# Identity products before waits that are foreseen, the page table at the fourth head, and an order written down, in a two-layer decoder step

## The chip, the cores and the metric

The kernel runs on one core of a Trainium2 chip. The metric is the device time of one launch in microseconds. A core has TensorE (matrix products into PSUM, an accumulator memory of eight banks), VectorE, ScalarE and GpSimd (elementwise work), SyncE (issues transfers), and DMA engines; each engine runs its own queue in order. ScalarE and GpSimd can issue transfers too.

## The reference

One inference step of two layers for a prompt of 512 tokens and eight samples of four tokens, width 1024, all in float32. Layer 0 mixes tokens with a gated linear recurrence (HGRN2, six heads of 128), layer 1 with sparse attention: an indexer scores all keys, the best 128 (prompt) or 256 (samples, over 1024 cached keys and the new ones) are chosen, and softmax attention runs over these. The samples' cached keys and values lie in pages that a page table names. Beside the mixer each layer has a cross-attention into 256 memory tokens, and behind it a gated MLP with a causal convolution of width 3.

```python
for layer in range(DEPTH):
    hp, hs = rms_norm(xp, norm_mix[layer]), rms_norm(xs, norm_mix[layer])
    if layer % N_MIXERS == 0:
        tp, sp = hgrn2_mixer(hp @ w_in_hgrn[j], s0, lower_bounds[j], hgrn_out_norm[j])   # and the samples
    else:
        ts = dsa_sample(qs, kn, vn, iqs, ikn, iws, cache_k[j], cache_v[j], cache_idx_k[j], page_table)
    xp = xp + jnp.concatenate([tp, cp], axis=-1) @ w_out[layer]
    fp, cvp = conv_ffn(rms_norm(xp, norm_ffn[layer]), ...)
    xp = xp + fp
```

## The kernel before

The stream is held feature-major, [128 features, 544 tokens] in eight tiles. A weight block of 128 x 1024 ("unit", 199 in all) is loaded by SyncE (in layer 1's mixer by GpSimd), cut by ScalarE into a rounded part `whi` and by VectorE or GpSimd into the rest `wlo`, and every product with the stream is three products of parts (`proj_fm`, lines 791 to 804): 48 products of 272 columns for one block of 128 features. Taking a unit into use cuts the unit two places later. An RMS norm is not applied before the product: `Norm._finish` (934 to 948) sums squares on TensorE, takes 1/sqrt by Newton steps on VectorE (`rsqrt`, 888), and turns the factor into rows by five transposes on TensorE (`rb`); the products are scaled as they leave PSUM (`scaled`, 950). In the MLP (`ffn`, 1180) the first gate and up blocks are computed before that factor is waited for.

The order of the instructions is made by the program. The main stream gives out the projections; beside it `Pump` (495) holds generators, each a chain of steps (a head's recurrence, a block of attention, a selection). Before each product of the main stream, `run` gives out all steps that `Model` (226), with a clock for each engine moved on by rough costs, holds ready; `finish`, `space` and `drain` do so until a generator ends or a tile is free. The same clocks choose the engine of some operations: VectorE or GpSimd for `wlo` (757), VectorE or ScalarE in `scale_rows` (861) and `scaled`. The program is made twice; the second time knows how often each tile is used.

Layer 0's mixer runs the parts of `MIX` (line 216): head 0, two blocks of values, the memory's keys and values, heads 1 to 4, another block of values, head 5, six gates. Then come the output projection (`out_proj`, 1172) and the MLP. Between the output projection and the MLP stand nine transfers of the page table, issued by ScalarE: 64 entries to all partitions (`ptb`, 1579) and, in eight pieces of 16 partitions, a strided copy (`ptv`, 1587), and on VectorE the six operations that make gather indices of them (`iidx`, `vidx`). The MLP of layer 0 gathers the index keys with `iidx`; layer 1 uses `vidx` and `ptb`.

Layer 1's mixer runs the parts of `ORDER` (line 217): index projections, memory loads, values, six queries, keys, then `attn` (adds the attention's generators), the memory's queries, and its keys and values. What is left of the attention is given out while the output projection waits for its inputs (`cat_ready`, 1168).

Of the kernel before, what the change touches and what calls it, by code (L numbers as in the profile page):

```python
# [33 lines left out]
# ---------------------------------------------------------------- host layout  # L34
# [43 lines left out]
def weight_units(i, order):  # L78
    """the weight blocks in the order in which the program asks for them"""
# [128 lines left out]
TURNS = 2          # selections at work at a time  # L208
# [10 lines left out]
ONACT = 4            # of a digit's seven thresholds, those that ScalarE counts  # L219
THRESHOLDS = 1, 2, 3, 4, 5, 6, 7  # L220

NUNITS = 199


class Model:
    """clocks of the engines (us), moved on by rough costs as instructions are given out, and the times from which
    tiles can be read: they decide which of the instructions at hand comes next"""
    LAT = dict(pe=0.2, act=0.14, dve=0.13, pool=0.1)     # from an instruction's end to a reader's start
    ROOM = dict(s=54, m=31, row=4, b=4)

    def __init__(self, plan=None):
        self.plan = plan                      # what an earlier pass wrote down; without it there is room for all
        self.uses, self.demand, self.pool, self.born, self.dies, self.held = {}, {}, {}, {}, {}, {}
        self.left, self.live = {}, dict.fromkeys(self.ROOM, 0)
        self.banks = [0.0] * self.ROOM["b"]   # times from which the free ones are free
        self.t = dict(pe=0.0, dve=0.0, act=0.0, pool=0.0, sp=0.0)
        self.dge, self.dma = [], []             # when the descriptor engine and the queues are busy
        self.ready, self.read, self.floor, self.rings = {}, {}, {}, {}
        self.whole = []
        self.lanes = [0.0] * 8, [0.0] * 8  # L240
        self.gen = None
        self.table, self.psum, self.mine, self.touch = 0, set(), {}, {}
        self.strict, self.keep, self.main = 2, 0, MAIN0
# [31 lines left out]
    def holds(self):  # L275
        """for each generator and step: the slots that it still takes at the most, and those that it gives back
        until its end"""
# [37 lines left out]
    def room(self, g, gens):  # L315
        """from when a generator's next step finds the tiles that it takes"""
# [12 lines left out]
    def ring(self, tag, n, name):  # L329
        """a tile takes the place of the one n allocations before it"""  # L330
# [11 lines left out]
    def held_up(self, n, eng):  # L342
        """until when other engines are at work on the part of a tile that is to be written"""
# [14 lines left out]
    def go(self, eng, cost, ins, outs):  # L358
# [3 lines left out]
        for n in outs:  # L362
            s = max(s, self.floor.get(n, 0.0))
            s = max(s, self.held_up(n, eng))
            if eng == "dve":
                s = max(s, self.mine.get(n, 0.0))
        e = self.t[eng] = s + cost
# [12 lines left out]
class Engine:  # L380
# [3 lines left out]
    def __getattr__(self, name):  # L384
        f = getattr(self._e, name)

        def call(*args, **kw):
# [9 lines left out]
            self._m.use(ins + outs)  # L397
            return f(*args, **kw)  # L398
# [3 lines left out]
def place(busy, t, took):  # L402
    """the first time from t on when something is free for so long"""
# [11 lines left out]
def extent(ap):  # L415
    """first and last column and partition of an operand in its tile"""
# [14 lines left out]
def cost(eng, model, name, args, kw, ins, outs):  # L431
    out = args[0] if args else kw["out"]
    n = size(out)
    if name in ("dma_start", "indirect_dma_start"):
        m = model
        at = m.t["pe"] if eng != "sp" or outs[0] not in m.floor else 0.0
        lanes = m.lanes[eng == "pool"]        # their completions are told apart by eight semaphores in turn
# [17 lines left out]
    if eng == "pe":  # L455
        l = args[1]
        load = size(l) * 0.107 / 128          # of the stationary operand, beside the product before
# [37 lines left out]
class Pump:  # L495
    """Generators of instructions beside the main stream. A generator yields, before each step, the tiles that
    the step reads (None: all that it has given out so far); a step is given out once they are ready."""
    def __init__(self, model):
        self.turn = 0
        self.m, self.gens, self.dv, self.names, self.urgent = model, [], [], {}, []  # L500

    def make(self, it, after=None, pri=0, margin=0):
        name = (self.m.gen.key + "_" if self.m.gen else "") + it.__name__
        self.names[name] = n = self.names.get(name, 0) + 1
        return Gen(it, after, f"{name}{n}", pri, margin)
# [12 lines left out]
    def ready(self, g):  # L518
# [5 lines left out]
        else:  # L524
            for n in g.need:
                if callable(n):                       # a condition, or a time
# [18 lines left out]
    def step_dve(self):  # L545
        """the streams take turns, so that one's instruction does not wait for its own one before"""
# [3 lines left out]
    def ahead(self):  # L550
        """steps of the DVE's own streams while it would otherwise wait"""
# [17 lines left out]
    def run(self, *need):  # L569
        """all steps that are ready; then, until the main stream's needs are ready, those that become so"""  # L570
# [13 lines left out]
    def idle(self):  # L584
        """nothing is ready: wait for what comes first; False if nothing can"""
# [14 lines left out]
    def finish(self, g):  # L600
        while not g.done:
# [8 lines left out]
    def space(self, tag):  # L610
        """the main stream's own tiles: it leaves some for the generators as long as they get on"""
# [8 lines left out]
    def drain(self):  # L620
        while self.gens:
# [3 lines left out]
def program(ctx, tc, a, pat, cat_, order, plan):  # L625
# [34 lines left out]
    def v3(ap, *dims):  # L660
        """[P, prod(dims)] -> [P, *dims]"""
# [53 lines left out]
    # ---- weights: loaded ahead in the order of their use, cut into two float32r parts  # L715
    class Weights:
        def __init__(self):
# [3 lines left out]
            self.whole = list(plan.whole) if plan else []       # units that are also used as they are  # L721
# [18 lines left out]
        def _cut(self):  # L740
# [12 lines left out]
            def part(c, n):  # L753
                S.activation(hi[:, c:c + n], raw[:, c:c + n], AF.Copy)
                late = max(model.t["pe"], model.t["pool"]) + self.lead
                (V if model.t["dve"] <= late else G).tensor_sub(lo[:, c:c + n], raw[:, c:c + n], hi[:, c:c + n].bitcast(F32))
# [3 lines left out]
            else:  # L760
                self.part = part              # the first unit is cut block by block
# [24 lines left out]
    def mm3(out, wh, wl, xh, xl, first, last):  # L786
        """out += x^T w, weights moving, both operands in two parts; three of the four products carry float32"""
# [3 lines left out]
    def proj_fm(blocks, xs, ks=None):  # L791
        """feature-major product: blocks() gives the next [128,128] weight parts, xs is a list of (hi, lo)"""
# [18 lines left out]
    def fm2(*name, xs, before=None, ks=range(8)):  # L811
        """two feature-major products, block by block"""
# [22 lines left out]
    def proj_tm(*name, xs):  # L835
        """token-major product with 256 columns, the results of the four prompt tiles and, for the samples, of
        the four blocks of a unit on 32 rows each"""
# [23 lines left out]
    def scale_rows(p, r):  # L861
        if model.t["act"] < model.t["dve"]:
# [10 lines left out]
    def split_in(src):  # L873
        """the two parts of a slot's contents as a generator"""
# [6 lines left out]
    def split2(src, parts, sl):  # L881
        """the same as a generator"""
# [5 lines left out]
    def rsqrt(v, out=None, p=128):  # L888
        """1/sqrt(v) by Newton steps on an integer first guess; v is overwritten"""
# [17 lines left out]
    # ---- residual stream, feature-major [d, token], and its norms: h holds x * gain in two parts,  # L907
    #      the factor 1/rms of a token is applied to the products
# [1304 lines left out]
```

## Time and profile before

| what | us |
|---|---|
| median of three runs (lowest, highest) | 1495.1 (1492.55, 1497.12) |
| span of the profiled execution | 1500.7 |
| TensorE busy in it | 1434.9 (96%) |
| VectorE, ScalarE, GpSimd busy | 803.2, 587.5, 567.3 |
| mean granted clock of TensorE, share of full | 0.978 |

The profiled execution is another one than the three timed ones; of its own time only the span from the first to the last instruction is given. Busy times overlap, since the engines run side by side. Layer 0's mixer takes about the first 287 us with its memory attention, its MLP begins at about 340 us; layer 1's mixer lies between about 747 and 1050 us, and its MLP follows from about 1102. The clock of TensorE is shown as a share of its full speed. All operations are recorded at one helper line (L398), so rows are told apart by their tiles: `a` is a projection's accumulator, `rb` and `rs` belong to a norm, `wlo` and `whi` to the weights.

### The profile page before, as it was taken

To read this page: it belongs to the slowest core of one execution; us is meant where nothing else is said; L and a number is where in the kernel's file an instruction comes from. 1 tells how busy PE (TensorE), PEld (TensorE's weight loads), DVE (VectorE), ACT (ScalarE), POOL (GpSimd) and SP (SyncE) were. 2 spreads that over 40 slices of the span, in tenths; PEclk is the share of its full clock that TensorE was granted. 3 is DMA by queue.
4 is the path that set the end of the run, shared out by engine and by line. 5 is a ranking of instruction groups with operands and counts; after the bars stand their busy time and mean duration, and the time that the engine had idled before them with its cause. 6 is when DMAs were issued, how large, how long until landed. Compare 5 with 4: busy or idle time off the path is not lost.

```text
span 1500.7 us, 28191 instructions
## 1 busy us (share of the span) xinstructions
PE 1434.9 (96%) x11314; PEld 1345.6 (90%) x11314; DVE 803.2 (54%) x1762; ACT 587.5 (39%) x1064; POOL 567.3 (38%) x600
## 2 busy tenths in 40 slices
PE   8989999998999999999999797689999999999998
PEld 7978889998999999999987775456999999999998
DVE  7466886653444234444469988867444442244431
ACT  5447466332333123333335443466333331133320
POOL 4422444323444124446753444341134440144410
PEclk9999999999999999999999997989999999999999
DMA  5542132321333223224414236631222323232241
GB/s 186 177 156 64 59 117 86 101 85 62 88 95 93 92 73 94 90 85 126 135 54 131 83 115 202 199 127 57 71 76 89 96 85 99 73 95 87 85 121 57
DMA packets 60145, 152.52 MB, mean 102 GB/s; under 512 B 9040, under 2 KB 22960, under 8 KB 60016
## 3 DMA queue, kind: packets, MB, share of 16 engines
q1 hardware_dynamic: 39456, 110.11, 23.9%
q0 software_dynamic: 8208, 26.50, 5.4%
q10 hardware_dynamic: 12352, 14.13, 2.9%
q8 instruction: 89, 1.46, 0.4%
q14 instruction: 40, 0.33, 0.1%
HBM read 142.23 MB, written 8.47 MB: 100 GB/s over the span
## 4 chain that ended last, share of the span: by engine, by line
PE 84%; DVE 11%; issue 2%; ACT 1%; DMA 1%; another core or an unknown queue 0%; ACTq 0%; POOL 0%; SPq 0%; DVEq 0%; POOLq 0%
PE a L398 71%; DVE ple_choose_sample L398 2%; PE u_hgrn_head L398 1%; DVE isc_index_prompt L398 1%; PE id_index_prompt L398 1%; PE mkv L398 1%; PE ao_prompt_attn L398 1%; PE ho_hgrn_head L398 1%; PE ms_prompt L398 1%; PE hgrn_head_samples L398 1%; PE as_prompt_attn L398 1%; DVE t L398 1%; DMA ptv<-pt 1%; DVE lo L398 1%; PE mo_prompt L398 1%
## 5 line engine op out<-in xcount | busy, mean ns | idle before, releaser
L398 PE MATMUL a<-hi,whi 128*128 128x272 f32 x2640 | 556.4, 292 | 1.4 <-DVE t L398 1.0
L398 PE MATMUL a<-lo,whi 128*128 128x272 f32 x2640 | 551.0, 290 | 4.9 <-DVE lo L398 4.6
L398 POOL TENSOR_TENSOR wlo<-raw,whi 128x1024 fp32r<-128x1024 f32 x143 | 342.7, 2397 | 557.3 <-ACT whi L398 551.1
L398 PE MATMUL a<-hi,wlo 128*128 128x272 f32 x2640 | 549.1, 289 | 0.0
L398 PEld LDWEIGHTS a<-hi,whi 128*128 128x128 f32 x2640 | 417.7, 190 | 9.2 <-issue 5.4
L398 PEld LDWEIGHTS a<-lo,whi 128*128 128x128 f32 x2640 | 418.1, 190 | 6.2 <-DVE lo L398 5.6
L398 PEld LDWEIGHTS a<-hi,wlo 128*128 128x128 f32 x2640 | 418.1, 190 | 0.0
L398 ACT ACTIVATE whi<-raw 128x1024 fp32r<-128x1024 f32 (+1 forms) x202 | 209.5, 1038 | 230.9 <-PE a L398 151.3
L398 DVE TENSOR_TENSOR wlo<-raw,whi 128x1024 fp32r<-128x1024 f32 (+1 forms) x59 | 79.7, 1351 | 160.6 <-ACT whi L398 157.7
L398 DVE TENSOR_TENSOR sc<-a,rb 128x544 f32<-128x544 f32 x53 | 38.4, 724 | 116.1 <-PE a L398 114.5
L398 DVE SCALAR_TENSOR_TENSOR conv<-ext,params,conv 128x560 f32<-128x560 f32 x88 | 70.6, 802 | 45.1 <-ACT conv L398 43.6
L398 DVE TENSOR_TENSOR ext<-a,rb 128x240 f32<-128x240 f32 x132 | 37.5, 339 | 105.9 <-PE a L398 102.2
L398 ACT ACTIVATE conv<-ext,params 128x560 f32<-128x560 f32 x44 | 37.6, 855 | 136.2 <-DVE ext L398 132.6
L398 ACT ACTIVATE hi<-sc 128x544 fp32r<-128x544 f32 x44 | 29.0, 658 | 137.3 <-DVE sc L398 137.3
L398 DVE TENSOR_TENSOR x<-a,x 128x544 f32<-128x544 f32 x48 | 34.7, 723 | 80.1 <-PE a L398 72.5
L398 POOL TENSOR_TENSOR sqa<-sqa,sq 128x544 f32<-128x544 f32 x24 | 34.8, 1448 | 110.0 <-ACT sq L398 108.3
L398 DVE TENSOR_TENSOR sc<-sc,conv 128x512 f32<-128x512 f32 x88 | 62.5, 748 | 4.9 <-DVE sc L398 0.5
L398 ACT ACTIVATE conv<-conv 128x560 f32<-128x560 f32 x44 | 29.6, 672 | 73.8 <-DVE conv L398 73.8
L398 ACT ACTIVATE hi<-x,params 128x544 fp32r<-128x544 f32 x32 | 23.9, 745 | 70.4 <-DVE x L398 68.5
L398 DVE TENSOR_TENSOR lo<-sc,hi 128x544 fp32r<-128x544 f32 x44 | 31.9, 725 | 31.9 <-ACT hi L398 31.9
L398 PE MATMUL a<-whi,hi 128*128 128x256 f32 x160 | 46.8, 293 | 0.0
L398 PE MATMUL a<-whi,lo 128*128 128x256 f32 x160 | 45.1, 282 | 0.0
(406 smaller groups left out, 1931.9 us busy)
## 6 DMA issues: line engine op xcount, KB each, us to landing
raw<-w SPq DMA_DIRECT2D x177, 512.0 KB, 3.6
raw<-w POOLq DMA_DIRECT2D x21, 512.0 KB
k_sample_scores<-ckT SPq DMA_DIRECT2D x46, 128.0 KB, 3.5
ck_mem_samples<-cmkT ACTq DMA_DIRECT2D x16, 256.0 KB, 6.2
cv_mem_samples<-cmv ACTq DMA_DIRECT2D x16, 256.0 KB, 4.7
st_s<-hgrn_head_samples POOLq DMA_DIRECT2D x12, 256.0 KB
hgrn_head_samples<-hst SPq DMA_DIRECT2D x10, 256.0 KB, 3.5
ck_sample_scores<-ckT SPq DMA_DIRECT2D x18, 128.0 KB, 2.1
```

The costliest lines, as they stand in the source:

```text
L398: return f(*args, **kw)
```

## The change

Three parts. First, the page table's nine transfers become a function that is called where head 3 of layer 0 begins, and the six index operations move ahead of the output projection. Second, the order of layer 1 is read from a string: letters name generators in the order in which they are made, a point ends the turn of `run`, `finish`, `space` or `drain`, and `+` or `-` answers a choice of engine (`pick`). Third, in layer 1's mixer up to the output projection, before the first product into a PSUM tile of 128 partitions (or a transpose) for which `Model` computes a wait of over 0.8 us, products of the identity with itself are given out that write the same tile.

```diff
+SCRIPT = (
+    "5.-A6.A2.-2.A8.-5.-2B2.B5.B3.-.B9.-4.B.B9.-CD6.3C.16C2E12CE2CE4CF4CE8CD2C4DFEF2D.-EFEDFH.HEF.E.FE.F.EF.EF.EF6.-I"
...
+    "-8.+8.+8.+8.-8.+24."
+)
 class Model:
+        if eng == "pe":
+            self.wait, self.last = s - self.last, s + cost
 class Engine:
             self._m.use(ins + outs)
+            out = args[0] if args else kw["out"]
+            if self._n == "pe" and self._m.fill and self._m.wait > 0.8 and out.shape[0] == 128 and (
+                    name == "transpose" or kw["start"]):
+                self._m.fill(out, self._m.wait)
             return f(*args, **kw)
 class Pump:
+    def begin(self, script):
+        self.made = [*self.gens, *self.dv]
+        self.script = iter([c for n, c in re.findall(r"(\d*)(\D)", script) for _ in range(int(n or 1))])
+    def play(self):
+        for c in self.script:
+            if c == ".":
+                return
+            g = self.made[LETTERS.index(c)]
+            self.step(g, self.gens if g in self.gens else self.dv)
+    def pick(self, c):
+        return c if self.script is None else next(self.script) == "+"
     def run(self, *need):
+        if self.script is not None:
+            return self.play()
...
-                (V if model.t["dve"] <= late else G).tensor_sub(lo[:, c:c + n], raw[:, c:c + n], hi[:, c:c + n].bitcast(F32))
+                (V if pump.pick(model.t["dve"] <= late) else G).tensor_sub(lo[:, c:c + n], raw[:, c:c + n], hi[:, c:c + n].bitcast(F32))
...
+    def page_table():
+        pt_ap = a["pt"]
+        S.dma_start(ptb, bass.AP(tensor=pt_ap.tensor, offset=pt_ap.offset, ap=[[0, 128], [1, 64]]))
+        for s in range(8):
+            S.dma_start(ptv[16 * s:16 * s + 16, :], bass.AP(tensor=pt_ap.tensor, offset=pt_ap.offset + s, ap=[[0, 16], [8, 8]]))
...
         hd = int(part)
+        if hd == 3:
+            page_table()
         f = fm("hfm", TOK + 128 * hd, xs=h)
...
+    if plan is not None:
+        pump.begin(SCRIPT)
     h = norm.h
...
+    def fill(out, us):
+        out = out[:, 0:min(size(out), 128)]
+        for _ in range(int((us - 0.4) / 0.224)):
+            nc.tensor.matmul(out, ident, ident[:, 0:size(out)], start=True, stop=True, skip_group_check=True)
+    model.fill = fill
     model.keep, model.main = KEEP, MAIN1
     for part in ORDER:
...
     W.queue, W.lead = Q, LEAD0
+    model.fill = None
```

## Rows read from the trace of the kernel before

**Rows 1.** The page: its span, and each engine's busy time.

```profile
span 1500.7 us, 28191 instructions
...
PE 1434.9 (96%) x11314; PEld 1345.6 (90%) x11314; DVE 803.2 (54%) x1762; ACT 587.5 (39%) x1064; POOL 567.3 (38%) x600
```

**Rows 2.** Windows: stretch, length, busy PE, PEld, DVE, ACT, POOL; clock, DMA, GB/s.

```profile
350.00:400.00 50.00, 47.43 (x359) 46.98 (x360) 23.93 (x55) 16.42 (x22) 19.19 (x26) 0.93 0.24 77
150.00:200.00 50.00, 47.85 (x446) 43.03 (x445) 42.38 (x113) 28.47 (x62) 22.27 (x26) 1.00 0.23 80
```

**Rows 3.** Windows of layer 1's mixer, with the same columns.

```profile
889.50:893.00 3.50, 3.50 (x26) 1.98 (x25) 3.03 (x16) 2.75 (x10) 0.00 (x0) 0.54 0.98 381
910.00:920.00 10.00, 5.42 (x18) 4.06 (x15) 9.75 (x35) 1.01 (x2) 4.28 (x6) 0.51 0.53 171
927.00:934.00 7.00, 5.85 (x20) 3.87 (x24) 4.44 (x18) 1.69 (x2) 1.68 (x4) 0.53 0.89 285
```

**Rows 4.** Waits, 340 to 400 us: total, times, longest, in us.

```profile
DVE vidx L398 <- DMA ptv<-pt: 10.0, 1, 10.0
...
PE rb__finish L398 <- DVE rs L398: 5.1, 1, 5.1
```

**Rows 5.** Timeline of TensorE, 346 to 358 us: start, length; idle time before in brackets.

```profile
352.57 1.36 PE L398 MATMUL rb__finish<-consts,rs 128*128 128x128 f32 x5 [5.05 <-DVE rs L398]
353.86 0.82 PE L398 MATMUL a<-hi,whi 128*128 128x272 f32 x2
...
357.83 0.41 PE L398 MATMUL a<-hi,whi 128*128 128x272 f32 x2
```

**Rows 6.** Windows of TensorE's work on `a` alone, from the norm's sums on, both MLPs.

```profile
339.76:379.76 40.00, 32.96 (x247) 0.91 0.22 71
...
1101.96:1141.96 40.00, 38.58 (x305) 1.00 0.27 80
```

**Rows 7.** Timeline of TensorE, layer 1's MLP: the factor's transposes.

```profile
1105.96 0.77 PE L398 MATMUL rb__finish<-consts,rs 128*128 128x128 f32 x5
```

**Rows 8.** The page table's tiles: count, shortest/median/longest in ns, first and last start.

```profile
L398 ACTq DMA_DIRECT2D ptv<-pt x8: 441/452/516, 336.2 to 339.7; - x8
...
L398 DVE TENSOR_SCALAR iidx<-ptb,consts x2: 233/238/242, 339.2 to 339.4; 64x32 int32<-64x32 int32 x2
```

**Rows 9.** Timeline of ScalarE, 138 to 215 us.

```profile
140.67 1.05 ACT L398 ACTIVATE whi<-raw 128x1024 fp32r<-128x1024 f32 x1
...
174.40 0.45 ACT L398 ACTIVATE oss_hgrn_head<-hgrn_head_samples 128x128 f32<-128x128 f32 x2 [6.52 <-PE hgrn_head_samples L398]
...
181.75 1.05 ACT L398 ACTIVATE whi<-raw 128x1024 fp32r<-128x1024 f32 x1
```

**Rows 10.** Waits of TensorE, 138 to 300 us: the only one.

```profile
PE u_hgrn_head L398 <- DVE km_hgrn_head L398: 2.2, 1, 2.2
```

**Rows 11.** SyncE: its wait in 336 to 345 us, and its timeline in 142 to 148.

```profile
SPq L398 <- DMA ptv<-pt: 7.5, 1, 7.5
...
144.27 0.33 SPq L398 DMA_DIRECT2D raw<-w  x1
```

**Rows 12.** Timeline of GpSimd at the end: a weight's second part.

```profile
1449.61 2.40 POOL L398 TENSOR_TENSOR wlo<-raw,whi 128x1024 fp32r<-128x1024 f32 x1 [12.53 <-ACT whi L398]
```

**Rows 13.** Waits of TensorE, 747 to 940 us.

```profile
PE qrb_query_scale L398 <- DVE rq L398: 3.3, 1, 3.3
PE mb_mem_samples L398 <- POOL rqx_mem_samples L398: 2.0, 1, 2.0
...
PE a L398 <- DVE t L398: 1.0, 1, 1.0
```

**Rows 14.** Float32 products, two records each: chain row at full clock, timeline row at half.

```profile
204.47 0.89 PE u_hgrn_head L398 x8
...
911.45 1.01 PE L398 MATMUL e_choose_sample<-ple_choose_sample,consts 128*128 128x2 f32 x4 [1.37 <-DVE ple_choose_sample L398]
```

**Rows 15.** Waits of VectorE, 885 to 951 us.

```profile
DVE p_prompt_attn L398 <- PE as_prompt_attn L398: 3.5, 1, 3.5
```

More of the change, by code (lines that the diff above doesn't have):

```diff
@@ L1 @@
+import re
 import numpy as np
@@ L222 @@
 NUNITS = 199
+LETTERS = "ABCDEFGHIJKLMNOPQRSTUVWXYZabcdefghijklmnopqrstuvwxyz!#$%&()*,/:;<=>?@[]^_{|}~"
+SCRIPT = (
+    "5.-A6.A2.-2.A8.-5.-2B2.B5.B3.-.B9.-4.B.B9.-CD6.3C.16C2E12CE2CE4CF4CE8CD2C4DFEF2D.-EFEDFH.HEF.E.FE.F.EF.EF.EF6.-I"
+    "2JHEHIJ.HF.E.FE.FE.FE.F.EF4.-2.J2H2.J3.J4.-2.J2H2.J3.J5.-2HK.K5.HEFH.K4.-2.2H10.-.2H15.-M2HL.L7.-HEFEHLM4.F.EFM"
+    "10.NMNJ2H.-VX2OZabcdePQRSTUW.J.OJ2.JHEFH2.J.2O.-2H.3J.J4.J6.2fOJ3.-f3JHJHJO.f.J6.-4J3OJEJFf3P3Q3R2S2T2U.2J6.-JPQ"
+    "STRU.S.EFJTU.EF.EP-3.-Q-JR+PS-T-U+fJ.QRPF2J.EfJFEfFQREJS.FE2f2PJ2Q2RP3SQT5.GRUglSFGFGJFP-Q-TGP2Tg3Jf.-JPQR+S-T3U"
+    "QfJF2GJfGPQT+U2WPVfPQP+RSU-VTgGQ2h2i2j2kP2G2RV-RSGSQ+VG2VGVPGRWQSTGR+2TXSQTRS+UWXR2GX+ST-3U4WTGUXGXG2XSGU+TGhiUh"
+    "jUGWi2Wh+-jki+-2h2WiGhj2-kW3Yih2-jijhk-+i2-jh3Gi3Yhi3G3Yij+-2kjGkGjG2P2Q2RP2SP+Q2TR2US2YPQ-TU3YQR-S-jk2-lYPZT-RU"
+    "-QZaSRZabTSabcUTbcdkUc.delkdel.k3.e3l9.+19.+11.+11.+11.+11.+11.+14.-m6.m2.-2.m10.-2.-10.-9.-2.-10.-9.-2.-10.-9.-"
+    "2.-10.-9.-2.-10.-9.-2.-10.-9.-2.-10.-9.-2.-10.-9.-2.-10.-9.-2.-10.-9.-2.-8.+8.+8.-8.+8.+8.+8.-8.+8.+8.+8.-10.-9."
+    "-2.-10.-9.-2.-10.-9.-2.-10.-9.-2.-10.-9.-2.-10.-9.-2.-10.-9.-2.-10.-9.-2.-10.-9.-2.-10.-9.-2.-10.-9.-2.-8.+8.+8."
+    "-8.+8.+8.+8.-8.+24."
+)
 class Model:
@@ L241, in __init__ @@
         self.gen = None
+        self.fill, self.wait, self.last = None, 0.0, 0.0
         self.table, self.psum, self.mine, self.touch = 0, set(), {}, {}
@@ L499, in __init__ @@
         self.turn = 0
+        self.script, self.made = None, []
         self.m, self.gens, self.dv, self.names, self.urgent = model, [], [], {}, []
@@ L504, in make @@
         self.names[name] = n = self.names.get(name, 0) + 1
-        return Gen(it, after, f"{name}{n}", pri, margin)
+        g = Gen(it, after, f"{name}{n}", pri, margin)
+        self.made.append(g)
+        return g
+    def begin(self, script):
[9 more added lines that the diff above has]
+        return c if self.script is None else next(self.script) == "+"
     def add(self, it, after=None, pri=5, margin=0):
@@ L600, in finish @@
     def finish(self, g):
+        if self.script is not None:
+            return self.play()
         while not g.done:
@@ L610, in space @@
     def space(self, tag):
+        if self.script is not None:
+            return self.play()
         m = self.m
@@ L620, in drain @@
     def drain(self):
+        if self.script is not None:
+            return self.play()
         while self.gens:
@@ L861, in scale_rows @@
     def scale_rows(p, r):
-        if model.t["act"] < model.t["dve"]:
+        if pump.pick(model.t["act"] < model.t["dve"]):
             S.activation(p, p, AF.Copy, scale=r)
@@ L951, in scaled @@
         t = slot(name="sc")
-        if model.t["dve"] > max(model.t["pe"], model.t["act"]) + BUSY:
+        if pump.pick(model.t["dve"] > max(model.t["pe"], model.t["act"]) + BUSY):
             S.activation(halves(t), ac, AF.Copy)
@@ L1542, in gate @@
         cat[hd] = yield from split_in(sg)
+    ptb = cp.tile([128, 64], I32, name="ptb")
+    ptv = cp.tile([128, 8], I32, name="ptv")
+    def page_table():
[3 more added lines that the diff above has]
+            S.dma_start(ptv[16 * s:16 * s + 16, :], bass.AP(tensor=pt_ap.tensor, offset=pt_ap.offset + s, ap=[[0, 16], [8, 8]]))
     memraw = []
@@ L1573, in program @@
         gens.append(pump.add(hgrn_head(hd, q, f, lb, m, lambda n: vts[n], ons), after=gens[hd - FLIGHT] if hd >= FLIGHT else None, pri=PRI["hg"], margin=MARGIN))
-    norm = Norm(gffn[:, 0, :])
-    out_proj(0, cat, [*([g] for g in gates), [mg[0], mg[1], mg[4]], mg[2:5]], norm)
-    n1 = Norm(gmix[:, 1, :])
-    ptb = cp.tile([128, 64], I32, name="ptb")
-    pt_ap = a["pt"]
-    S.dma_start(ptb, bass.AP(tensor=pt_ap.tensor, offset=pt_ap.offset, ap=[[0, 128], [1, 64]]))
     iidx = cp.tile([128, 32], I32, name="iidx")
@@ L1585, in program @@
         V.tensor_scalar(iidx[pr], p4[pr, :, e], 64.0, cc("iota64")[pr], op0=ALU.mult, op1=ALU.add)
-    ptv = cp.tile([128, 8], I32, name="ptv")
-    for s in range(8):
-        S.dma_start(ptv[16 * s:16 * s + 16, :], bass.AP(tensor=pt_ap.tensor, offset=pt_ap.offset + s, ap=[[0, 16], [8, 8]]))
     vidx = cp.tile([128, 4, 8], I32, name="vidx")
@@ L1592, in program @@
         V.tensor_scalar(vidx[:, i, :], vidx[:, 0, :], float(i), None, op0=ALU.add)
+    norm = Norm(gffn[:, 0, :])
+    out_proj(0, cat, [*([g] for g in gates), [mg[0], mg[1], mg[4]], mg[2:5]], norm)
+    n1 = Norm(gmix[:, 1, :])
     def gather(out, src, idx):
```

## The prediction

> **What bounds the kernel now.** I read the page first: it puts TensorE's busy share of the 1500.7 us at 96% [rows 1], so time goes where TensorE stands still or runs at its lower clock. The windows come next. Three places concern this change: the start of layer 0's MLP (350 to 400 us: TensorE 47.43 of 50 busy, mean granted clock 0.93) and the stretch where head 3 begins (150 to 200: 47.85 busy, VectorE 42.38) [rows 2], and layer 1's mixer, where the clock is low again and again while VectorE is full (9.75 of 10 us in 910 to 920) [rows 3]. The waits of 340 to 400 us name the cause in the first: VectorE stands 10.0 us for the last page-table transfer, and TensorE 5.1 us for the norm factor that is queued behind this on VectorE [rows 4]. The chain of waits runs through the same transfer.
>
> **The page table moves.** *Removed, in layer 0's MLP.* The index operations sit on VectorE ahead of the norm's Newton steps; without them these follow the sums at once. The timeline of TensorE shows what the delay costs: 5.05 us idle before the five transposes of the factor, these 1.36 us long, and then products at two thirds to half speed (a pair takes 0.82, 0.41 once the clock is back) until 357.8 us [rows 5]. The clock was at 2.4 GHz, fell to 1.2 GHz after the idle time, and rose again. The price of the whole is read from the same step in layer 1, where nothing stands before the norm: in the 40 us from the sums on, TensorE does 305 products there and 247 here, 38.58 us for 305, that is 0.126 each [rows 6]. 58 products x 0.126 = 7.3 us. It agrees with the pieces: 5.05 idle, 0.6 on the transposes (1.36 against 0.77 [rows 7]), 1.6 on some 16 products at half speed. What is late next is known from layer 1 too: the transposes follow the products without idle time, so nothing takes the stall's place. Lower bound of the gain: 5.05, if another low clock comes; upper: 7.3. I take 7.3.
>
> *Added, at head 3 in layer 0.* Nine transfers are issued by ScalarE just before head 3's first product: some 9 x 0.45 = 4.1 us with what lies between them [rows 8]. Each unit of weights that is taken into use has the cut of the one two places later ahead of it; counted back from the third block of values, head 3's first is taken with the cut at 140.67 us [rows 9], and the nine come just before, ahead of this cut, the copies out of the memory attention and head 2's activations. ScalarE next stands idle for long before 174.4 us (6.52 us [rows 9]), so up to there what it feeds may be late. The cut is for a block that comes into use two units later and has time; the copies release PSUM and feed VectorE, which is almost full there. The trace holds no such hold-up in the mixer, so bounds: nothing, if TensorE has products of heads 2 and 3 to do meanwhile (the planner of layer 0 is still at work and counts ScalarE late by about as much, so it gives those out first); 4.1 idle and 2.2 for the lower clock as after the idle time at 350 us (0.6 + 1.6 above), 6.3, if all of it reaches TensorE; below nothing, -2.2, if the new order avoids the one wait of 2.2 us that TensorE has there [rows 10]. I take +1.5: nearer the busy TensorE row than the full hold-up. The transfers' own way: SyncE stood 7.5 us behind them in the stretch from 336 us. At 144.27 SyncE issues a weight load [rows 11]; the same wait would put it to about 152, for a block that ScalarE cuts some 30 us later, at 181.75 [rows 9]: nothing.
>
> The Trainium skill ("DMA: Bandwidth & Descriptors", "Issuing engines are not separate DMA queues") says that transfers of ScalarE and SyncE end up on the same engines and interleave, which speaks against putting these beside head 3's weight and state loads. The 7.5 us of SyncE agree that one issuer's small transfers hold up another's. By the rule a load is late; by the slack of 30 us it costs nothing.
>
> *The index operations.* Six, the longest of 0.24 us [rows 8], at most 1.4 us, go ahead of the output projection, whose VectorE work waits for TensorE; their data has landed long before. 0, at most 1.4.
>
> **The order written down.** Read mark by mark, the string gives out layer 1 exactly as the planner of before does: the same 975 turns of the main stream, the same generator steps between, the same 36 and 122 choices of engine. The trace shows this where a choice has its own row: the string's last marks are + + - + + + - +, and the last eight weight parts of the trace are cut on VectorE twice, on GpSimd (1449.61), then three on VectorE, one on GpSimd, one on VectorE [rows 12]. 0, with no bound on either side but the fills.
>
> **The fills.** They are 128 x 128 products of float32 identities, before the first product into a PSUM tile of 128 partitions (or a transpose) where the program's own clocks see a wait over 0.8 us, (wait - 0.4)/0.224 each. They act only until the output projection begins, at about 951 us here; the waits of the attention after that get none. In the trace the longest waits that qualify are 3.3 us (query scale) and 2.0 (memory queries), and there is one of 1.0 for an accumulator [rows 13]: 12 + 7 + 2 = 21 products if the clocks saw them as the chip has them; with the shorter ones and waits that the chip doesn't have I allow 20 to 40. One costs 0.22 us (four in 0.89), 0.45 at the lower clock (two of the same kind 1.01) [rows 14]. Cover: the waits themselves. Not covered: the accumulator's, because a fill writes the very bank whose release is awaited and so starts after the wait (2 x 0.22 = 0.45); and any that the clocks foresee where the chip has no wait, such as the turn of the keys.
>
> What they give back: the low stretches within their reach are 889.5 to 893 (clock 0.54), 910 to 920 (0.51) and 927 to 934 (0.53) [rows 3]. (1 - clock) x length is 1.6, 4.9 and 3.3. The second is free: VectorE is busy 9.75 of 10 and TensorE 5.42, so VectorE sets the pace. The others, 4.9 together, are on the path: VectorE stands 3.5 us for the score products that come at the end of the last stretch [rows 15]. Bounds: -4.9; and +8.8 for 40 uncovered products at 0.22, +18 at 0.45. I take -1.0: a fifth of the gain kept after 0.5 of uncovered fills and half a microsecond where fills outlast the 2.0 us wait. The Trainium skill ("TensorE: Matmul & The Clock Gate", "HAM oscillation — how this bites in real kernels") counts half of all throttled time as lost. By it these stretches would give back half of 20.5 us, 10; the row that shows VectorE full takes the middle one out of that.
>
> **Sum.** -7.3 + 1.5 + 0 + 0 - 1.0 = -6.8 us. Of the profiled execution only the span is given, 1500.7, 3.6 above the slowest of the three timed runs (1492.55 to 1497.12); so the difference is carried to the median: 1495.1 - 6.8 = **1488.3**.
>
> **Rivals.**
> 1. *ScalarE's hold-up at head 3 reaches TensorE.* For: VectorE is nearly full and takes its input from ScalarE there. Against: TensorE waits but once between 138 and 300 us. -7.3 + 6.3 - 1.0: 1493.1.
> 2. *The fills hold the clock up.* For: the low stretch of 927 to 934 follows the wait of 2.0 us that is filled. Against: fills take a third of the 3.3 us wait if foreseen short. -7.3 + 1.5 - 4.9: 1484.4.
> 3. *The stall's place is taken.* The MLP's weight parts or accumulators are late instead, half of 7.3 goes. For: the idle row there names only what came last, and a second lateness can lie behind it. Against: layer 1's rows. -3.7 + 1.5 - 1.0: 1491.9.
> 4. *The fills lie on the path: slower.* They wait for the bank, run at the lower clock, and the queue is in order, so scores, memory keys and VectorE behind them are late. 40 x 0.45 = 18, less the 5.8 of the table: 1507. It decides from 13 uncovered fills at the lower clock or 26 at the upper. For: the clock is low in 17 of the 24 us from 910 to 934. Against: most are put where TensorE has an idle row.
>
> **How the numbers follow.** Forecast 0.50, rival 1 0.18, rival 2 0.14, rival 3 0.10, rival 4 0.08. The forecast's own range is 1485 to 1491.5. The range for 8 in 10 leaves out rival 4 and the edges of 2 and 1: 1481.5 to 1495.0. 0.3% of 1495.1, 4.5 us, is what a measurement here can tell from no change: faster is below 1490.6. Faster: nearly all of rival 2 and 0.46 of the forecast with little of rival 3, 0.63; same: rivals 1 and 3 and the forecast's rest, 0.28; slower 0.09.
>
> **What would show it.** The wait of VectorE for the page table is gone and the transposes of layer 0's MLP factor follow about 4 us after the sums without idle time; the windows behind stay at clock 1.00. ScalarE shows nine issues near 141 us and TensorE's idle time in 138 to 175 stays below 4 us. Between 820 and 951 us there are 20 to 40 identity products; the clock of 927 to 934 tells rival 2 from the forecast. From 1050 us on the kernel takes as long as before. The forecast fails if layer 0 ends over 4 us later than before, or if TensorE's fills stand where it had no idle time.

## The result, and the profile after: slower by half a per cent

The changed kernel takes **1502.2 us** (median of 12 runs, 1499.65 to 1504.9), the kernel before 1494.2 on the same chip (12 runs, 1488.2 to 1497.12): a ratio of **1.0056, 95% interval 1.0043 to 1.0068**. It is slower by 8 us where 6.8 us less was forecast.

The page of the changed kernel: its span and each engine's busy time, against [rows 1].

```profile
span 1501.1 us, 28288 instructions
...
PE 1446.2 (96%) x11370; PEld 1358.1 (90%) x11370; DVE 816.5 (54%) x1763; ACT 586.1 (39%) x1063; POOL 566.1 (38%) x599
```

The spans of the two profiled executions hardly differ, since before's is 6.5 us above its median and the changed kernel's 1.1 below. So the stages are compared, each from the sums of one norm (the first `st__finish` product) to the next:

| stage, us | before | after | difference |
|---|---|---|---|
| up to layer 0's first norm | 26.0 | 26.7 | +0.7 |
| layer 0's mixer and output projection | 313.4 | 328.6 | **+15.2** |
| layer 0's MLP | 407.6 | 399.7 | **-7.9** |
| layer 1's mixer and output projection | 354.8 | 346.2 | -8.6 |
| layer 1's MLP | 398.9 | 400.0 | +1.1 |

All but layer 1's mixer add up to +9.1, about what the medians show. Layer 1's mixer varies most between profiles of one kernel (the changed kernel has 346.2 here and 360.4 on another chip, e5 below); it is left to the experiments.

**The MLP of layer 0 did what was foreseen.** Windows of the changed kernel with the columns of [rows 2]: from 350 us on TensorE is busy all the time at full clock, where before had 47.43 and 0.93. The second row is `a` alone from the sums on: 306 products in 40 us, against 247 [rows 6].

```profile
350.00:400.00 50.00, 50.00 (x407) 49.76 (x405) 22.09 (x48) 17.60 (x23) 18.94 (x23) 1.00 0.28 89
```

```profile
355.25:395.25 40.00, 38.58 (x306) 1.00 0.25 80
```

The timeline of TensorE there: the factor's transposes come 4.15 us after the sums, without idle time, and take 0.77 us instead of 1.36 [rows 5].

```profile
355.24 1.12 PE L419 MATMUL st__finish<-consts,sqa 128*128 128x1 f32 x16
...
359.14 0.41 PE L419 MATMUL a<-hi,wlo 128*128 128x272 f32 x2
359.39 0.77 PE L419 MATMUL rb__finish<-consts,rs 128*128 128x128 f32 x5
```

**The mixer of layer 0 lost twice that.** Windows of the whole stage, up to 138 us (just before head 3) and from there on; first the kernel before:

```profile
25.99:138.00 112.01, 107.86 (x849) 94.11 (x849) 65.59 (x171) 57.07 (x118) 36.87 (x40) 0.98 0.42 135
138.00:339.39 201.39, 199.24 (x1742) 185.33 (x1737) 140.68 (x337) 107.12 (x215) 77.25 (x69) 1.00 0.27 86
```

and the changed kernel, with the 50 us in which head 3 begins [rows 2]:

```profile
26.65:138.00 111.35, 107.32 (x825) 93.27 (x824) 62.65 (x166) 54.11 (x112) 36.86 (x40) 0.95 0.40 131
138.00:355.25 217.25, 208.47 (x1765) 191.65 (x1764) 156.55 (x348) 109.55 (x221) 75.64 (x69) 0.98 0.26 83
```

```profile
150.00:200.00 50.00, 46.20 (x392) 40.63 (x392) 41.96 (x97) 26.27 (x58) 18.86 (x18) 0.93 0.18 60
```

Two numbers of such a row say what it loses: length less busy TensorE is idle time, and (1 - clock) x length what the lower clock costs. The clock is shown to 0.01, so the second number is good to about 1 us in such a stretch. From 138 us on, before has 2.1 + 0.0, the changed kernel 8.8 + 4.3. What is left of the stage once both losses are taken off in both parts is 304.9 before and 305.9 after: the same work. So some 11.0 of the 15.2 us are new waits of TensorE, and the low clock behind them, from head 3 on. Another 3.3 are low clock ahead of 138 us (5.6 against 2.2), where both kernels give out the same instructions; the runs below show anything from 2.2 to 6.7 there, whatever their order, so it is put down to chance.

The waits of TensorE from 138 to 305 us (total, times, longest). Before has one, of 2.2 [rows 10]:

```profile
PE ot_hgrn_head L419 <- DVE o_hgrn_head L419: 2.0, 1, 2.0
PE hgrn_head_samples L419 <- DVE km_hgrn_head L419: 1.9, 1, 1.9
PE ho_hgrn_head L419 <- DVE hgrn_head_samples L419: 1.5, 1, 1.5
PE sc_hgrn_head L419 <- DVE k_hgrn_head L419: 1.2, 1, 1.2
PE u_hgrn_head L419 <- ACT on_hgrn_head L419: 0.9, 2, 0.7
```

Only the fourth stands near ScalarE's nine issues, and e2 below has it without them. The issues are there, at 142 us; the timeline of ScalarE:

```profile
142.09 0.33 ACTq L419 DMA_DIRECT2D ptb<-pt  x1
142.46 0.45 ACTq L419 DMA_DIRECT2D ptv<-pt  x1
...
144.38 2.86 ACTq L419 DMA_DIRECT2D ptv<-pt  x6
147.29 1.06 ACT L419 ACTIVATE whi<-raw 128x1024 fp32r<-128x1024 f32 x1 [3.53 <-PE mpt_prompt L419]
```

Right behind them the order on TensorE is another. Before (timeline of TensorE), three rows of head 3's f projection, six products, stand between the memory attention's transposes and its last products:

```profile
143.10 0.50 PE L398 MATMUL a<-hi,whi 128*128 128x272 f32 x2
...
143.69 0.41 PE L398 MATMUL a<-hi,wlo 128*128 128x272 f32 x2
144.04 2.00 PE L398 MATMUL mo_prompt<-mpt_prompt,mv 128*64 128x256 f32 x16
```

In the changed kernel it is 18 rows, 36 products, from 146.10 on: five blocks more, since three rows are a block of the product. The attention's last products and head 2's recurrence (`sc_hgrn_head`) come behind them, and then TensorE has to wait:

```profile
146.10 0.50 PE L419 MATMUL a<-hi,whi 128*128 128x272 f32 x2
...
150.45 0.41 PE L419 MATMUL a<-hi,wlo 128*128 128x272 f32 x2
150.79 2.00 PE L419 MATMUL mo_prompt<-mpt_prompt,mv 128*64 128x256 f32 x16
152.72 0.65 PE L419 MATMUL mot_join<-consts,mo_mem_samples 128*128 128x128 f32 x4
153.22 0.39 PE L419 MATMUL sc_hgrn_head<-sc,kd_hgrn_head 128*128 128x128 f32 x2
154.83 0.33 PE L419 MATMUL sc_hgrn_head<-consts,k_hgrn_head 128*128 128x128 f32 x1 [1.23 <-DVE k_hgrn_head L419]
```

The planner has been told of nine issues on ScalarE, some 4.3 us by its own costs, holds the generators' steps behind ScalarE for not ready, and gives out these five blocks ahead of them. From there on the order of layer 0 is new: of the 1554 turns, steps and choices of engine that the planner makes for it, the first 333 are as before.

Three of the four longest waits stand right behind VectorE operations that took several times their usual length beside operations of GpSimd; the rows are in the last section. The fourth, the 1.5 us at 223 us, has GpSimd idle.

### The profile page after: what moved, and what is told of

It reads as the page before. It is cut to its first block, busy times and chain, and to the rows that moved or that the text cites. A ratio compares the mean times of both kernels' runs of the same rounds, so it can differ in the third digit from the quotient of the medians.

```text
span 1501.1 us, 28288 instructions
## 1 busy us (share of the span) xinstructions
PE 1446.2 (96%) x11370; PEld 1358.1 (90%) x11370; DVE 816.5 (54%) x1763; ACT 586.1 (39%) x1063; POOL 566.1 (38%) x599
## 4 chain that ended last, share of the span: by engine, by line
PE 81%; DVE 13%; ACT 3%; issue 2%; DMA 1%; POOL 0%; SPq 0%; DVEq 0%; ACTq 0%; POOLq 0%
PE a L419 70%; DVE ple_choose_sample L419 2%; PE mkv L419 1%; DVE isc_index_prompt L419 1%; DVE m_hgrn_head L419 1%; PE id_index_prompt L419 1%; PE u_hgrn_head L419 1%; PE ms_prompt L419 1%; PE as_prompt_attn L419 1%; DVE sc L419 1%; DVE t L419 1%; PE ho_hgrn_head L419 1%; DMA raw<-w 1%; DVE mpt_choose_prompt L419 1%; PE hgrn_head_samples L419 1%
```

## The experiments

The kernel before takes some 1494 us on the first chip and 1510 to 1513 on the others, so each ratio is against the kernel before on the same chip. In the diffs `+` is what is added to the changed kernel. Two readings were set against each other first: *the issues* (ScalarE's time at head 3 holds up what TensorE needs) and *the order* (the planner's answer to them costs, even where nothing is issued).

**e5, the changed kernel again**, on a second chip.

> After itself, on the chip of the three beside it. Theory A as the last runs leave it (new order of layer 0 +11, wait in the MLP -7.3, fills nothing): 1.002 to 1.004 of before. If the first comparison, 1.0056, holds and the fills cost what is left: 1.005 to 1.007.

Measured: 1519.5 against 1513.0, ratio 1.0035 [1.0022, 1.0048]; layer 0's stage 330.8, its MLP 400.4. The loss is there on another chip too.

**e1, the same issues, unseen by the planner.** ScalarE issues the nine transfers at the same place, but not through the object that charges the clocks, so layer 0 keeps before's order.

```diff
-        S.dma_start(ptb, ...)
+        nc.scalar.dma_start(ptb, ...)
-            S.dma_start(ptv[...], ...)
+            nc.scalar.dma_start(ptv[...], ...)
```

> After, but the nine transfers at head 3 are issued past the planner's clocks, so layer 0 keeps the order that it had before; the transfers stand on ScalarE at head 3 all the same. Theory A (the new order of layer 0, which the planner makes since it counts ScalarE late, costs the 15 us between the two norms' sums): the distance from layer 0's first sums to its MLP's sums returns from 328.6 to about 314 us, and the time falls to 1484 to 1489. Theory B (ScalarE's hold-up itself costs it): the distance stays over 322 us and the time at 1498 to 1503. Theory C (the fills cost it): 1498 or more with the distance back at 314.

Measured: 0.9951 [0.9935, 0.9968], faster than before. Stage 320.7, MLP 400.4; from 138 us on 3.9 idle and 2.1 of low clock. With 3.3 us more of low clock ahead of 138 us than before (0.95 against 0.98), these losses make up the 7.3 us by which the stage is over before's 313.4.

**e2, the order alone.** An engine that issues nothing is charged with the nine transfers at head 3; the real ones and the index operations go back to their old place, and there are no fills.

```diff
+class Ghost:
+    def __getattr__(self, name):
+        return lambda *args, **kw: None
...
         if hd == 3:
-            page_table()
+            page_table(Engine(Ghost(), "act", model, cost))
...
+    page_table(S)           # after out_proj, as before
...
-    model.fill = fill
+    model.fill = None
```

> Before's place for the transfers and the index operations, no fills, layer 1's order as written; but the planner's clocks are charged with nine transfers at head 3 that are not issued, so layer 0 gets the new order and nothing holds ScalarE. Theory A: the distance between the two sums is 322 to 329 us and the time 1504 to 1510, since the 7.3 us wait in the MLP is still there. Theory B: distance about 314, time 1492 to 1497.

Measured: 1.0074 [1.0059, 1.0089]. Stage 329.1, MLP 409.0. Nothing is issued at head 3, and the waits of TensorE are nearly the changed kernel's, in the same places (2.0, 1.9, 1.6, 1.2, 0.9). With e1 this settles it: the order, not the issues.

**e6, SyncE issues them**, unseen by the planner (`nc.sync.dma_start` in e1's two lines).

> As the run that keeps layer 0's order, with the nine transfers at head 3 issued by SyncE and past the planner's clocks, so ScalarE is not held up either. If the hold-up of ScalarE is what made layer 0 320.7 us there against 315.0 with the transfers in the MLP: layer 0 at 314 to 316 us, ratio 0.990 to 0.993. If that difference was the clock's chance: 0.994 to 0.997, layer 0 still at 318 to 321. If weight or state loads behind the nine on SyncE are late: slower than that, with TensorE or ScalarE waiting for a load at 145 to 165 us.

Measured: **0.9935 [0.9910, 0.9959]**, the lowest ratio of the study, about 10 us under before (e1, and e11 and e15 below, lie within its interval). Its window from 138 us on, with the columns as above, keeps 2.15 us of idle time, before's:

```profile
138.00:345.21 207.21, 205.06 (x1771) 190.24 (x1770) 147.47 (x349) 112.37 (x225) 79.80 (x71) 0.99 0.28 87
```

ScalarE's hold-up in the old order is at most the 1.7 us of idle time that e1 has more; the ratios of e1 and e6 don't tell them apart.

**e8 and e9, the charge elsewhere**: as e2, but `if hd == 2` and `if hd == 5`.

> As the run with the order alone, but the planner is charged with the nine transfers at head 2, where it gives out another order again; nothing is issued there, and the MLP's wait stands. If counting ScalarE late is a bad rule wherever it is applied: 1.006 or more. If the orders are a lottery: anything from 0.995 to 1.008, with TensorE's idle time in layer 0 going with it.

> As the run with the order alone, but the planner is charged at head 5, the last, where less than half of layer 0's mixer is left to be ordered anew; nothing is issued there, the MLP's wait stands, no fills. If a charge that puts one projection ahead of the heads costs by what is left to order: 1.002 to 1.006, under the 1.0074 of head 3 and the 1.0153 of head 2. If it is a lottery: it can as well be below 1.000.

Measured: at head 2 1.0153 [1.0132, 1.0174], stage 339.3; at head 5 1.0025 [1.0001, 1.0048], stage 322.5.

**e13 and e14, a smaller charge at head 3**: as e2, with two and five transfers charged. The expectations of both count the blocks that are pulled ahead as one, three to four and, for e2, seven. In the traces 6, 12 and 18 rows stand where before has three, so it is one, three and five.

```diff
-    def page_table(S):
+    def page_table(S, pieces=8):
-        for s in range(8):
+        for s in range(pieces):
-            page_table(Engine(Ghost(), "act", model, cost))
+            page_table(Engine(Ghost(), "act", model, cost), 1)     # e14: 4
```

> As e2 (transfers and index operations at their old place, no fills, only the planner of layer 0 charged at head 3), but with a charge of two transfers instead of nine, which moves one block of head 3's f projection ahead instead of seven. If the cost of the new order grows with the blocks pulled ahead: layer 0 some 2 us over the kernel before (about a seventh of e2's 14), ratio 1.000 to 1.002. If any new order of layer 0 costs what the old one had gained by being picked: layer 0 some 8 to 16 us longer, ratio 1.004 to 1.009.

> As e13, with a charge of five transfers, which moves three to four blocks ahead. Growth with the blocks: layer 0 some 6 to 8 us longer than before's, ratio 1.003 to 1.005, between e13 and e2. Any new order costs the same: 8 to 16 us, ratio 1.004 to 1.009, with no order among e13, e14 and e2. If both e13 and e14 come out at or below 1.000, then neither holds, and it is the pulling ahead of all of head 3's product alone.

Measured: e13 1.0046 [1.0028, 1.0064], stage 324.2; e14 1.0014 [0.9998, 1.0029], stage 320.1. Their windows from 138 us on, e13 first:

```profile
138.00:350.70 212.70, 204.82 (x1753) 188.69 (x1752) 158.67 (x341) 104.82 (x218) 69.11 (x66) 0.98 0.26 84
```

```profile
138.00:346.85 208.85, 205.31 (x1772) 189.22 (x1772) 151.04 (x345) 110.95 (x224) 73.96 (x68) 1.00 0.28 86
```

Neither reading of the two holds as written: one block pulled ahead costs 6.9 us (0.0046 x 1510), three cost 2.1 (the interval reaches from -0.3 to 4.4), five 11.2. The cost doesn't grow with the blocks, and new orders don't all cost the same. What it does follow, in one profile of each, is what TensorE loses in the trace from 138 us on:

| kernel (order alone) | idle + low clock, us | over before's 2.1 | ratio | in us |
|---|---|---|---|---|
| e14, five charged at head 3 | 3.5 + 0.0 | 1.4 | 1.0014 | 2.1 |
| e9, nine at head 5 | 4.5 + 4.2 | 6.6 | 1.0025 | 3.8 |
| e13, two at head 3 | 7.9 + 4.3 | 10.1 | 1.0046 | 6.9 |
| e2, nine at head 3 | 9.0 + 4.4 | 11.3 | 1.0074 | 11.2 |
| e8, nine at head 2 | 13.7 + 6.8 | 18.4 | 1.0153 | 23.1 |

**e4, fills and written order without the move**: `page_table()` is called after `out_proj`, and the index operations stand there.

> The page table and the index operations at before's place, layer 0's order as before, layer 1's order as written, and the fills. Fills worth 8.6 us: 1485 to 1488. Worth nothing: 1492 to 1496. Theory C: 1500 or more.

Measured: 0.9995 [0.9981, 1.0009]. Layer 0's stage is 315.0 and its MLP 407.9, before's lengths within 2 us. From layer 1's norm on, the trace has before's instructions on every engine in before's order, and 56 records of fills between them.

**e3, e11 and e15, no fills** (`model.fill = None`): e3 is otherwise the changed kernel, e11 is e10 below, e15 is e6.

> After without the identity products. If these are worth the 8.6 us that layer 1's mixer is shorter by in the profiles (354.8 to 346.2 from its norm's sums to the MLP's): 1509 to 1512. If the profile of before was an unlucky one in layer 1: 1500 to 1504, level with after. If they cost (theory C): 1495 or less.

> The same without the identity products. Fills worth nothing (as before with fills alone, 0.9995): within 0.0015 of the run beside it. Fills that keep the clock up: 0.003 or more above it. Fills that cost: 0.003 or more below it.

> The changed kernel with its nine transfers issued by SyncE at head 3 outside the planner's clocks (as e6, layer 0 in its old order), and without the fills. If the fills lie on the path beyond the waits: ratio 0.990 to 0.993, some 2 to 4 us under e6's 0.9935. If they are free: 0.9935 as e6. If they hold the clock up: 0.995 to 0.997. MLP of layer 0 at 400.5 us and its rb not waited for in all three.

Measured: e3 1.0028 [1.0018, 1.0038] (e5, with fills, 1.0035); e11 0.9943 [0.9922, 0.9965] (e10 0.9968); e15 0.9946 [0.9926, 0.9965] (e6 0.9935). The expectation of e15 that fits is the one in which the fills are free, but its interval covers the others' edges. The intervals overlap in all three pairs: 28 fills change the time by less than these runs can tell. The single profiles don't settle it: on the later chips layer 1's mixer takes 360.4 to 363.4 us in the six kernels with 28 fills (e1, e4 to e7, e10) and 352.3 to 361.4 in seven of the eight without (365.1 in e8); on the first chip it is 346.2 with fills and 354.8 without.

**e10, the issues at a gate; e12, three times the fills; e7, the index operations behind the output projection.** The nine transfers are issued by ScalarE, unseen by the planner, ahead of the third gate, where the heads' work is nearly given out.

```diff
             hd = len(gates)
+            if hd == 2:
+                page_table()          # with nc.scalar.dma_start
...
-        for _ in range(int((us - 0.4) / 0.224)):
+        for _ in range(3 * int((us - 0.4) / 0.224)):      # e12 only
```

> Layer 0's order kept; the nine transfers issued by ScalarE at the third gate past the planner's clocks; the index operations ahead of the output projection, as in after; fills. If the loss of after is the new order and the hold-up at head 3 and nothing else: layer 0 at 314 to 317 us, the MLP at 400, ratio 0.990 to 0.9935. If a part of the table's gain is lost wherever the transfers stand: 0.995 or more.

> The same with three times as many identity products at each place, 84 for 28. If they lie in TensorE's waits and VectorE sets the pace there: within 0.002 of the run with 28, since what goes beyond a wait is taken up by the next one. If they lie on the path: the 56 more at 0.22 us, less some 3 us of waits that still have room, add 6 to 12 us, 0.004 to 0.008. If more of them hold the clock up: faster by 0.002 or more.

> Layer 0's order kept, the nine transfers issued by ScalarE at the third gate, where it stands idle most of the time, past the planner's clocks; index operations after the output projection. Theory A: layer 0 at 314 to 316 us, the MLP at 400, ratio 0.990 to 0.993. If any nine issues on ScalarE cost 4 to 6 us wherever they stand: 0.994 to 0.997.

Measured: e10 0.9968 [0.9948, 0.9987], stage 316.0, MLP 400.5. The two lengths are those of the first expectation, the ratio that of the second; e11, the same without fills, has 0.9943, so what e10 lacks is not settled. e12 1.0036 [1.0020, 1.0053]: 56 more products cost 0.0068 x 1513 = 10.3 us, as expected for fills that lie on the path. The windows of 900 to 950 us, e10 and then e12: TensorE does more, VectorE gets 10 us less done in this stretch (over the whole of layer 1's mixer it is busy for 268 us, as against 270), and the clock is lower, not higher.

```profile
900.00:950.00 50.00, 42.59 (x299) 32.80 (x297) 44.35 (x155) 19.46 (x49) 19.57 (x23) 0.86 0.65 207
```

```profile
900.00:950.00 50.00, 45.21 (x305) 40.06 (x304) 33.95 (x114) 9.96 (x17) 16.80 (x21) 0.77 0.57 178
```

e7, which leaves the index operations behind the output projection, is at 0.9990 [0.9979, 1.0002] with an MLP of 404.8: though the data are long there, half of the gain is lost, which neither expectation had. TensorE waits 2.5 us for the factor. On VectorE, ahead of the Newton steps, the two `iidx` operations take 2.60 us and one Newton step 2.32; GpSimd is at a weight's second part both times. First VectorE, then GpSimd (timelines):

```profile
341.49 2.60 DVE L419 TENSOR_SCALAR iidx<-ptb,consts 64x32 int32<-64x32 int32 x2
...
346.22 2.32 DVE L419 SCALAR_TENSOR_TENSOR rs<-m__finish,rs 128x5 f32<-128x5 f32 x1
```

```profile
341.14 2.66 POOL L419 TENSOR_TENSOR wlo<-raw,whi 128x1024 fp32r<-128x1024 f32 x1 [5.56 <-ACT whi L419]
346.18 2.35 POOL L419 TENSOR_TENSOR wlo<-raw,whi 128x1024 fp32r<-128x1024 f32 x1 [2.38 <-ACT whi L419]
```

## Why the prediction was wrong

- **The page table out of layer 0's MLP: right.** 7.3 us forecast, 7.9 in the profile, 407.6 to 399.7; e4, with the table at its old place, has 407.9. Nothing took the stall's place (rival 3).
- **"Added, at head 3 in layer 0": the step that failed.** It was sized at +1.5 with an upper bound of 6.3. The bounds were made for a hold-up of ScalarE, and for that they hold: with the old order (e1) there are 1.7 us more of idle time and 2.1 of low clock than before. What the step left out is in its own sentence, that the planner "counts ScalarE late by about as much, so it gives those out first". This was taken as a help, and below nothing as its best case. It is the loss: some 11 us in the profile, 11.2 in e2 where nothing is issued. In the new order VectorE's operations meet GpSimd's, and TensorE waits for them, on which the prediction has no term. So the upper bound was no bound: it came from one instruction's delay, while the edit changes the order of the whole rest of the mixer.
- **Rival 1 was beside the point**, though it stood on the right line: its mechanism, the hold-up, is not what the runs show. TensorE loses 1.2 us in 140 to 165 (e2 has the same wait, without the issues); the larger waits end at 184, 224 and 287 us.
- **The index operations: 0, right for the time, wrong in the working.** Two of them took 3.72 us instead of 0.49, beside work of GpSimd (below). Ahead of the output projection nothing waits for that; behind it, e7 shows the price.
- **The written order: 0, right.** The traces have before's order from layer 1's norm on, on every engine (e4).
- **The fills: -1.0 forecast, nothing measured.** There are 28 of them, within the 20 to 40 (the trace has two records for each). 14 stand before `mb`, where 7 were counted, and 5 before the query scale, where 12 were; these 19 write 32 columns each, not 128. e4's ratio bounds them together with the written order to -2.9 to +1.4 us. Rival 2 (they hold the clock) and rival 4 (18 us on the path) both fail for this number; e12 shows rival 4's cost at three times the number, and against rival 2 a clock that falls. Rival 4's price of 0.45 does not follow from its row: 1.01 us for two is 0.5 each, and those products have 2 columns.
- **The sum.** With the order's 11 in the place of 1.5 and the fills at 0, the steps give -7.9 + 11 = +3.1. The ratios say +8.4 here (0.0056 x 1494), +5.3 in e5 and +4.2 in e3. The rest, 1 to 5 us, is not settled; the low clock ahead of 138 us and layer 1's mixer both move by as much between executions.

The sign that was named as what would make the forecast fail is the one that came: layer 0's sums stand at 355.24 us, 15.8 later than before.

What makes one order better than another is read from the traces and not tested: how often VectorE's operations meet GpSimd's. In layer 0's stage VectorE is busy for 206.3 us before, for 212.2 and 213.1 in the two cheaper orders of the table (e14, e9), and for 218.6 to 222.8 in the three dearer ones (e2, e8, e13). In e2 these are 507 instructions as before, one weight part more among them, so nearly all of the 12.3 us is longer operations; in e8 and e13 VectorE also cuts five weight parts more (19 against 14). Within the three the busy time does not rank the costs, and no run keeps GpSimd out of the way, so the account stays open there. No count made ahead of a run (blocks pulled ahead, place of the charge) ranked the orders.

## What to carry to other kernels

Where a planner with modelled clocks makes the order, an instruction that it is told of can change all that comes after it: price such an edit as a new order of unknown worth, with bounds from what TensorE's waits could be there, and not as one more instruction. Before a transfer is moved, take it out of the planner's sight or keep the order fixed, so that the move is all that changes; here this turns a loss of 0.35% into a gain of 0.65% on one chip (e5, and e6 with SyncE as the issuer), and without a change of the issuer a loss of 0.28% into a gain of 0.49% on another (e3, which has no fills, and e1).

This planner's `Model` moves the clocks of VectorE and GpSimd on independently of each other, so it cannot foresee that one holds up the other: look for small VectorE operations that have become long before a new order is trusted.

Products put into waits are worth a test against none and against three times as many, since a wait that is foreseen need not be there.

## What the runs showed of the hardware that was not expected

**Small VectorE operations can take ten times their time beside GpSimd.** The two `iidx` operations take 0.49 us before, with GpSimd idle, and 3.72 in the changed kernel (VectorE, then GpSimd; timelines):

```profile
302.87 3.72 DVE L419 TENSOR_SCALAR iidx<-ptb,consts 64x32 int32<-64x32 int32 x2
306.60 0.23 DVE L419 TENSOR_SCALAR vidx<-ptv,consts 128x8 int32<-128x8 int32 x1
```

```profile
302.84 1.35 POOL L419 TENSOR_TENSOR sc<-sc,rb 128x544 f32<-128x544 f32 x1 [4.93 <-ACT sc L419]
304.16 2.39 POOL L419 TENSOR_TENSOR wlo<-raw,whi 128x1024 fp32r<-128x1024 f32 x1
```

The two end within 0.04 us of the ends of GpSimd's (304.19 and 306.55), and the next, 0.23 us, runs once GpSimd stands. The Trainium skill ("SBUF — State Buffer", "SBUF: two separate sides") says that the two engines share one pair of ports, that whichever starts first holds it for its whole instruction, and that the other is blocked, not slowed; of VectorE's operations it names those in a two-port mode and those with two SBUF inputs. The rows agree with the lock: GpSimd's `sc` starts 0.03 us ahead of the first of them. In e7 this is worth about 4 us of the MLP (404.8 against 400.5).

**The same stands in front of TensorE's new waits.** Three operations of the heads before (views of their tiles, 138 to 340 us: shortest, median and longest in ns):

```profile
L398 DVE TENSOR_TENSOR k_hgrn_head<-k_hgrn_head,sc x5: 717/725/726, 145.6 to 259.1; 128x544 f32<-128x544 f32 x5
L398 DVE TENSOR_TENSOR m_hgrn_head<-m_hgrn_head,m_hgrn_head x15: 165/166/177, 175.8 to 284.4; 128x5 f32<-128x5 f32 x15
L398 DVE TENSOR_TENSOR sc<-sc,on_hgrn_head x6: 714/716/725, 252.4 to 291.0; 128x544 f32<-128x544 f32 x6
```

and in the changed kernel, ahead of the waits that end at 154.8, 183.8 and 287.4 us (VectorE, then GpSimd; timelines):

```profile
151.88 2.90 DVE L419 TENSOR_TENSOR k_hgrn_head<-k_hgrn_head,sc 128x544 f32<-128x544 f32 x1
178.93 2.31 DVE L419 TENSOR_TENSOR m_hgrn_head<-m_hgrn_head,m_hgrn_head 128x5 f32<-128x5 f32 x1
283.61 2.89 DVE L419 TENSOR_TENSOR sc<-sc,on_hgrn_head 128x544 f32<-128x544 f32 x1
```

```profile
151.84 2.36 POOL L419 TENSOR_TENSOR wlo<-raw,whi 128x1024 fp32r<-128x1024 f32 x1 [0.80 <-DMA ptv<-pt]
178.82 2.40 POOL L419 TENSOR_TENSOR wlo<-raw,whi 128x1024 fp32r<-128x1024 f32 x1
283.06 2.86 POOL L419 TENSOR_TENSOR wlo<-raw,whi 128x1024 fp32r<-128x1024 f32 x1
```

Each time GpSimd starts first, and VectorE's operation ends 0.02 to 0.6 us after GpSimd's. Ahead of the second wait four operations of VectorE in a row are held in this way, from 177.57 to 183.76 us; the one shown is the second of them. The hold-ups (2.2, 2.1 and 2.2 us) are longer than the waits behind them (1.2, 2.0 and 1.9). e2 has the three of them too, at the same places. Before's only wait of TensorE there stands behind the same: two `sc` operations of VectorE take 3.95 us from 155.70 on, beside GpSimd's work up to 159.60.

**A wait of 2 us can cost more than itself.** Windows of the changed kernel around the longest new wait: TensorE is busy for 0.18 of 2 us while VectorE is full, and then runs at about half of its full clock (1.2 GHz instead of 2.4) for some 6 us, though it is nearly full again from 186 us on.

```profile
182.00:184.00 2.00, 0.18 (x2) 0.19 (x3) 1.97 (x4) 0.00 (x0) 1.21 (x2) 1.00 0.00 0
184.00:186.00 2.00, 1.61 (x7) 1.13 (x7) 1.66 (x6) 0.31 (x2) 0.00 (x0) 0.53 0.00 0
186.00:188.00 2.00, 2.00 (x11) 1.98 (x10) 0.49 (x2) 1.99 (x3) 0.00 (x0) 0.50 0.00 0
188.00:190.00 2.00, 1.83 (x9) 1.46 (x8) 1.89 (x6) 0.67 (x2) 0.00 (x0) 0.50 0.00 0
```

Before's only wait there, 2.2 us [rows 10], has no low clock behind it (1.00 from 138 us on). So a wait of this length may or may not be followed by one, and a bound for a new wait has to hold both.
